# Row maxima of the attention scores from 64-row matmuls in two halves of the array

## The chip, the cores and the metric

The kernel runs on one core of a Trainium2 chip. The metric is the device time of one execution in microseconds (us). A profiled execution also has a span, the time from its first to its last instruction. TensorE is called PE here, VectorE DVE, ScalarE ACT, GpSimd POOL, and SyncE (which only issues transfers) SP. PE's weight loads have a row name of their own, PEld.

## The reference

Two layers of a transformer trunk work on 128 context tokens and 512 latent tokens of width 1024. Each layer has two groups of attention heads, then a gated feed-forward block. The change touches the attention alone, and of it this function and its twin:

```python
def diff_attend(q, k, v, lam):          # layer 0, 4 heads of two 64-wide maps each
    scale = q.shape[-1] ** -0.5
    def block(qb):
        s = jnp.einsum('bqhcd,bthcd->bhcqt', qb, k).astype(jnp.float32) * scale
        p = jax.nn.softmax(s, axis=-1)
        ...
def gqa_attend(q, k, v):                # layer 1, 8 query heads over 2 key heads, 64 wide
    ...
        s = jnp.einsum('bqkgd,btkd->bkgqt', qb, k).astype(jnp.float32) * scale
        p = jax.nn.softmax(s, axis=-1).astype(v.dtype)
```

For each latent query there are 640 keys (512 latent ones and 128 of a cache). A softmax is the same whatever number is subtracted from a row of scores, so the number that stands for the row's maximum may be a little off.

## The kernel before

**Numbers in two parts.** Most products run in the float32r type. A value is split in a high and a low part, and three products (high by high, high by low, low by high) are summed. For 64-wide heads the parts are stacked, so that one matmul over 128 rows of the array does two of the three: rows 0 to 63 of a tile `q1..` hold the high part, rows 64 to 127 the high part of q and the low part of k. A second tile `q2..` holds the rest and, in one extra row, the negated maxima.

**Pairs.** `attention` works through eight pairs per layer; a pair has two maps (`m` is 0 or 1). In layer 0 these are D0 to D3 (the differential heads) and M0 to M3 (96-wide latent heads); in layer 1 G0 to G3 (grouped-query heads) and N0 to N3 (neighbourhood heads, whose maxima take another path, `near`).

**Maxima.** `max_steps` gives eight steps for a pair, one for each map and each quarter `qt` of the 512 queries (function `one`). A step takes a PSUM tile `pm` of two banks, makes two matmuls of 320 keys each over all 128 rows with the same 128 queries as weights (L530), and DVE reduces 640 columns to one (L531). `fin` transposes the eight columns with one matmul (`pmx`), ACT negates them, and two small transfers (L554, `q<-att`) lay them into the extra row of the second tile.

**Scores and values.** The `st` tiles hold scores (L574, 512 queries wide), ACT takes their exponentials (L586), POOL sums them, and `po` tiles take the products with the values (L643). In layer 0's D pairs a `po` matmul has 128 output columns; in the M and G pairs it has 64, and the two maps stand in the two halves of the array's columns. `qs` (L719) holds the scores of the context tokens: 64 rows of the array, map 0 on rows 0 to 63, map 1 on rows 64 to 127. `ada` (L326) is filler work of the next modulation, 32 columns wide, with its weights in `wm`.

**Order.** The loop in `attention` mixes, by the strings in `CFG`, the maxima of pair i+1 (x), the scores of pair i (s) and the values of pair i-1 (v). A scheduler then orders each engine's instructions by their simulated readiness; PE, DVE, ACT, POOL and the SP queue each work in that order. The last two input projections of each layer (`peq`, `pek` in layer 0, `pnq`, `pnk` in layer 1; 128 rows, L186) run between the first pair's maxima. All transfers into the `q` tiles (L843 to L847 in `place64`, L1276 and L1277 for the G pairs) go through the SP queue (`PLACE`).

Of the kernel before, what the change touches and what calls it, by code (L numbers as in the profile page):

```python
# [11 lines left out]
F32R = mybir.dt.float32r  # L12
AF = mybir.ActivationFunctionType
ALU = mybir.AluOpType
AX = mybir.AxisListType
# [29 lines left out]
CFG = {"att0": ('xxsv', 4, 1, True, 2), "att1": ('vsxx', 4, 0, True, 2)}  # L45
TAIL = {"att0": 7, "att1": 9}
CUTS = {"op": 352, "dl": 352, "end": 384}
NCST = 5204
FULL = {5: 2, 8: 3}
KEEP = {5: 2, 8: 0}  # L50
NA_RANGES = [(0, 192), (64, 320), (192, 448), (320, 512)]
# [5 lines left out]
def tile_step(ctx: ExitStack, tc: tile.TileContext, a: dict):  # L57
    nc = tc.nc
    PE, ACT, DVE, POOL, SP = nc.tensor, nc.scalar, nc.vector, nc.gpsimd, nc.sync
# [7 lines left out]
    def dr(name, dt=F32):  # L67
        return dw(name, dt)[:, 0:1280]
# [4 lines left out]
    def d2(t):  # L73
        return t.rearrange("p (a b) -> p a b", a=2)

    def pmm(name):
        return pp.tile([128, 1024], F32, tag="mm", name=name, bufs=2)
# [3 lines left out]
    def psm(name, kind="sm"):  # L81

        tag, bufs = banks[kind]
        return pq.tile([128, 512], F32, tag=tag, name=name, bufs=bufs)
# [19 lines left out]
    def ring(tag, cols, bufs, dt=F32):  # L104

        if tag not in rings:
            rings[tag] = [0, [place([128, cols]) for _ in range(bufs)]]
        r = rings[tag]
        r[0] += 1
        v = r[1][(r[0] - 1) % bufs]  # L110
        return v if dt is F32 else v.bitcast(dt)
# [6 lines left out]
    def bf(t):  # L118
        return t.bitcast(F32)
# [6 lines left out]
    SPILL, SWAP, PLACE, OUT = POOL, ACT, SP, ACT  # L126
# [392 lines left out]

    def max_steps(pr):  # L520

        mx = ring("mx", 8, 2)

        def one(m, qt):
            mp = pr.maps[m]
            pt = pmm(f"pm{pr.name}{m}{qt}")
            ql = mp.qmax[:, qt * 128 : (qt + 1) * 128]
            col = mx[:, m * 4 + qt : m * 4 + qt + 1]
            for hf in range(2):
                PE.matmul(pt[:, hf * 512 : hf * 512 + 320], ql, mp.kmax[:, hf * 320 : hf * 320 + 320], start=True, stop=True)  # L530
            DVE.reduce_max(col, d2(pt)[:, :, 0:320], axis=AX.XY)  # L531

        def near(m, qts):

            mp = pr.maps[m]
            pt = pmm(f"pm{pr.name}{m}{qts[0]}")
            for i, qt in enumerate(qts):
                s, e = NA_RANGES[qt]
                n = e - s
                ql = mp.qmax[:, qt * 128 : (qt + 1) * 128]  # L540
                o = pt[:, 512 * i : 512 * i + 128 + n]
                PE.matmul(o[:, 0:128], ql, mp.kmax[:, 512:640], start=True, stop=True)
                PE.matmul(o[:, 128:], ql, mp.kmax[:, s:e], start=True, stop=False)
                PE.matmul(o[:, 128:], mp.ident, mp.combS[:, NA_COMB[qt] : NA_COMB[qt] + n], start=False, stop=True)
            c0, step = m * 4 + qts[0], qts[1] - qts[0]
            DVE.reduce_max(mx[:, c0 : c0 + step + 1 : step], d2(pt)[:, :, 0 : 128 + n], axis=AX.X)

        def fin():
            pm = psm(f"pmx{pr.name}")
            PE.matmul(pm[0:8, 0:128], mx, ident, start=True, stop=True)  # L550
            mr = pr.att.mr[pr.idx % 2][0:8].bitcast(F32R)
            ACT.activation(mr, pm[0:8, 0:128], AF.Copy, scale=-1.0)
            for m, mp in enumerate(pr.maps):
                PLACE.dma_start(bf(mp.maxrow), bf(mr[4 * m : 4 * m + 4, :]))  # L554

        if pr.na:
            return [lambda m=m, q=q: near(m, q) for m in range(2) for q in ((0, 3), (1, 2))], fin
        return [lambda m=m, qt=qt: one(m, qt) for m in range(2) for qt in range(4)], fin

    def score_steps(pr):  # L560
# [277 lines left out]

    def place64(slots, H, Lo, m):

        a1, a2 = slots.next()
        rs = slice(64 * m, 64 * m + 64)
        PLACE.dma_start(bf(a1[0:64, 0:1152]), H[rs, 0:1152])  # L843
        PLACE.dma_start(bf(a1[64:128, 0:512]), H[rs, 0:512])
        PLACE.dma_start(bf(a1[64:128, 512:1152]), Lo[rs, 512:1152])
        PLACE.dma_start(bf(a2[0:64, 0:512]), Lo[rs, 0:512])
        PLACE.dma_start(bf(a2[0:64, 512:1152]), H[rs, 512:1152])  # L847
        mp = Obj()
        mp.maxrow = a2[64:65, 0:512].rearrange("p (t q) -> p t q", t=4)
        mp.qmax, mp.kmax = a1[:, 0:512], a1[:, 512:1152]  # L850
        mp.passes = [(a1[:, 512:1152], a1[:, 0:512]), (a2[0:65, 512:1152], a2[0:65, 0:512])]
        return mp

    def new_pair(name, na, diff, dim, of):
        pr = Obj()
        pr.name, pr.na, pr.diff, pr.scale, pr.of = name, na, diff, dim ** -0.5, of
        pr.maps, pr.after = [], None
        return pr
# [53 lines left out]
    def mixer_even(u, o, fill, tail, pts):  # L912
# [9 lines left out]
        for j in range(4):  # L922
            t = {}
# [31 lines left out]
        pt = pmm("pkpe")  # L955
# [86 lines left out]
        for j in range(2):  # L1042
            cc = slice(512 + j * 128, 640 + j * 128)
            pt = pmm(f"pqr{j}")
# [67 lines left out]
        def mla_job(j):  # L1112
            def load():
                pr = new_pair(f"M{j}", False, False, 96, o[j])
                for m in range(2):
                    hd = 2 * j + m
                    a1, a2 = slots.next()
                    rs = slice(64 * m, 64 * m + 64)
                    rr = slice(32 * (hd % 4), 32 * (hd % 4) + 32)
                    qc = (hd // 4) * 512  # L1120
                    PLACE.dma_start(bf(a1[0:64, 0:1152]), mH[j][rs, 0:1152])
                    PLACE.dma_start(bf(a2[0:64, 0:1152]), mL[j][rs, 0:1152])
                    PLACE.dma_start(bf(a1[64:96, 0:512]), rH[rr, qc : qc + 512])
                    PLACE.dma_start(bf(a2[64:96, 0:512]), rL[rr, qc : qc + 512])
                    PLACE.dma_start(bf(a1[64:96, 512:1152]), kHL[:, 0:640])
                    PLACE.dma_start(bf(a2[64:96, 512:1152]), kHL[:, 640:1280])
                    DVE.memset(bf(a1[96:97, 512:1152]), 1.0)
                    mp = Obj()
                    mp.maxrow = a2[96:97, 0:512].rearrange("p (t q) -> p t q", t=4)
                    mp.qmax, mp.kmax = a1[0:96, 0:512], a1[0:96, 512:1152]  # L1130
                    mp.passes = [(a1[0:96, 512:1152], a1[0:96, 0:512]), (a2[0:96, 512:1152], a1[0:96, 0:512]), (a1[0:97, 512:1152], a2[0:97, 0:512])]
                    mp.ctx = [
                        (mctx[rs, j * 128 : j * 128 + 128], mctx[rs, 512 + j * 128 : 640 + j * 128]),
                        (mctx[rr, 1024 + (hd // 4) * 128 : 1152 + (hd // 4) * 128], kpc[rr, 0:128]),
                    ]
                    mp.v = lambda kt, hd=hd: vkt(vm, kt)[:, hd * 64 : hd * 64 + 64]
                    pr.maps.append(mp)
                return pr

            return load  # L1140
# [11 lines left out]
    def mixer_odd(raw, o, fill, tail, first, h):  # L1152
# [7 lines left out]
        gK = scratch("gK", [128, 1280])  # L1160
# [14 lines left out]
        for j in range(4):  # L1175
            t = {}
# [81 lines left out]
        kk, masks, lows = [], [], []  # L1258

        def gqa_job(j):  # L1260
            def load():
                if j == 0:
                    for g in range(2):
                        rs = slice(64 * g, 64 * g + 64)
                        t = dr(f"gk{g}", F32R)
                        PLACE.dma_start(bf(t[0:64, 0:640]), gK[rs, 0:640])
                        PLACE.dma_start(bf(t[64:128, 0:640]), gK[rs, 640:1280])
                        PLACE.dma_start(bf(t[0:64, 640:1280]), gK[rs, 0:640])
                        DVE.memset(bf(t[64:65, 640:1280]), 1.0)
                        kk.append(t)  # L1270
                pr = new_pair(f"G{j}", False, False, 64, o[j])
                g = j // 2
                for m in range(2):
                    rs = slice(64 * m, 64 * m + 64)
                    t, _ = slots.next(False)
                    PLACE.dma_start(bf(t[0:64, 0:1024]), gQ[j][rs, :])  # L1276
                    PLACE.dma_start(bf(t[64:128, 0:512]), gQ[j][rs, 0:512])  # L1277
                    mp = Obj()
                    mp.maxrow = t[64:65, 512:1024].rearrange("p (t q) -> p t q", t=4)
                    mp.qmax, mp.kmax = t[:, 0:512], kk[g][:, 0:640]  # L1280
                    mp.passes = [(kk[g][:, 0:640], t[:, 0:512]), (kk[g][0:65, 640:1280], t[0:65, 512:1024])]
                    mp.ctx = [(gctx[rs, 128 * j : 128 * j + 128], kctx[rs, 128 * g : 128 * g + 128])]
                    mp.v = lambda kt: vkt(vn, kt)[:, 512 + 64 * g : 576 + 64 * g]
                    pr.maps.append(mp)
                return pr

            return load
# [449 lines left out]
```

## Time and profile before

| what | value |
|---|---|
| time, median of 3 runs | 1895.18 us (1889.68, 1895.18, 1895.63) |
| time of the profiled execution | 1889.26 us |
| its span | 1887.1 us |
| PE busy | 1823.5 us, 97% of the span |
| DVE, ACT, POOL busy | 54%, 43%, 10% |
| mean granted TensorE clock | 0.975 of full speed |

The span and the profiled execution's time are to be read together (2.2 us lie around the span). PE's busy time counts matmuls with modelled ends, so a busy PE may still be waiting inside a row.

### The profile page before, as it was taken

To read this page: it belongs to the slowest core of one execution; us is meant where nothing else is said; L and a number is where in the kernel's file an instruction comes from. 1 tells how busy PE (TensorE), PEld (TensorE's weight loads), DVE (VectorE), ACT (ScalarE), POOL (GpSimd) and SP (SyncE) were. 2 spreads that over 40 slices of the span, in tenths; PEclk is the share of its full clock that TensorE was granted. 3 is DMA by queue.
4 is the path that set the end of the run, shared out by engine and by line. 5 is a ranking of instruction groups with operands and counts; after the bars stand their busy time and mean duration, and the time that the engine had idled before them with its cause. 6 is when DMAs were issued, how large, how long until landed. Compare 5 with 4: busy or idle time off the path is not lost. (4 is left out here: it accounts for less than half of the span.)

```text
span 1887.1 us, 29009 instructions
## 1 busy us (share of the span) xinstructions
PE 1823.5 (97%) x11715; PEld 1578.8 (84%) x11715; DVE 1014.7 (54%) x1782; ACT 803.6 (43%) x1325; POOL 190.2 (10%) x199
## 2 busy tenths in 40 slices
PE   7999799999999999999999999999999999999997
PEld 4888555559899999999989985455989999999996
DVE  3454445463774564663666654435377456466365
ACT  3433233345654452442475523324465444244244
POOL 0011243340000000000000003630000000000000
PEclk8999799999999999999999998999999999999998
DMA  7546555224223324333233364573412222222213
GB/s 283 167 147 224 140 173 143 77 95 162 79 85 97 126 78 145 128 114 107 97 101 131 131 197 141 162 200 114 168 68 100 91 68 67 82 75 62 85 58 105
DMA packets 84102, 229.88 MB, mean 122 GB/s; under 512 B 12225, under 2 KB 24897, under 8 KB 83969
## 3 DMA queue, kind: packets, MB, share of 16 engines
q1 hardware_dynamic: 74656, 209.73, 34.6%
q0 software_dynamic: 2592, 10.49, 1.5%
q10 hardware_dynamic: 6720, 7.82, 1.5%
q8 instruction: 92, 1.51, 0.3%
q14 instruction: 42, 0.34, 0.1%
HBM read 198.82 MB, written 28.06 MB: 120 GB/s over the span
## 5 line engine op out<-in xcount | busy, mean ns | idle before, releaser
L186 PE MATMUL pu<-uop,wh_u 128*128 128x322 f32 (+1 forms) x2688 | 512.6, 312 | 0.0
L186 PEld LDWEIGHTS pu<-uop,wh_u 128*128 128x128 f32 x2688 | 428.4, 190 | 5.8 <-ACT wh_u L160 4.1
L186 PE MATMUL pu<-uop,wl_u 128*128 128x322 f32 x1344 | 308.3, 311 | 0.0
L1361 DVE SCALAR_TENSOR_TENSOR za<-za,cst 128x127 f32<-128x127 f32 (+1 forms) x528 | 193.2, 435 | 92.1 <-ACT za L1353 91.8
L186 PEld LDWEIGHTS pu<-uop,wl_u 128*128 128x128 f32 x1344 | 224.8, 188 | 0.0
L186 PE MATMUL dn<-g,wh_d 128*128 128x320 f32 x1088 | 204.5, 309 | 0.1
L186 PEld LDWEIGHTS dn<-g,wh_d 128*128 128x128 f32 x1088 | 171.0, 188 | 0.9 <-ACT wh_d L160 0.9
L160 ACT ACTIVATE wh_u<-wr_u 128x1024 fp32r<-128x1024 f32 x88 | 92.9, 1058 | 138.3 <-PE dn L186 66.8
L271 POOL TENSOR_TENSOR cst<-cst 128x3 f32<-128x3 f32 (+2 forms) x23 | 24.8, 1077 | 1222.7 <-DVE cst L269 1220.0
L186 PE MATMUL dn<-g,wl_d 128*128 128x320 f32 x544 | 124.1, 309 | 0.0
L161 DVE TENSOR_TENSOR wl_u<-wr_u,wh_u 128x1024 fp32r<-128x1024 f32 x88 | 107.3, 1219 | 21.7 <-ACT wh_u L160 18.4
L442 ACT ACTIVATE za<-za,cst 128x128 f32<-128x128 f32 (+1 forms) x176 | 89.4, 555 | 38.3 <-DVE za L440 37.1
L186 PEld LDWEIGHTS dn<-g,wl_d 128*128 128x128 f32 x544 | 91.0, 188 | 0.0
L160 ACT ACTIVATE wh_d<-wr_d 128x768 fp32r<-128x768 f32 (+1 forms) x48 | 38.6, 809 | 103.8 <-PE dn L186 92.0
L1353 ACT ACTIVATE za<-za,cst 128x640 f32<-128x640 f32 x88 | 81.2, 923 | 3.0
L160 ACT ACTIVATE g<-za 128x640 fp32r<-128x640 f32 x44 | 32.5, 739 | 115.2 <-DVE za L1392 115.2
L439 DVE COPY cst<-pu 128x2 f32<-128x2 f32 x88 | 13.8, 157 | 123.7 <-PE pu L186 116.7
L1408 DVE TENSOR_TENSOR yf<-yf,dn 128x640 f32<-128x640 f32 x32 | 26.3, 821 | 94.8 <-PE dn L186 94.7
L1387 ACT ACTIVATE za<-za 128x640 f32<-128x640 f32 x44 | 32.5, 739 | 94.3 <-DVE za L1361 94.3
L440 DVE TENSOR_TENSOR za<-pu,rnuop 128x640 f32<-128x640 f32 x88 | 71.8, 816 | 0.0
L326 PE MATMUL ada<-wm,cst 128*32 128x256 f32 x768 | 64.0, 403 | 4.0 <-DMA wm<-in_wmod 2.0
L161 DVE TENSOR_TENSOR wl_op<-wr_op,wh_op 128x1024 fp32r<-128x1024 f32 x26 | 31.7, 1224 | 56.1 <-ACT wh_op L160 56.1
(585 smaller groups left out, 3424.2 us busy)
## 6 DMA issues: line engine op xcount, KB each, us to landing
wm<-in_wmod SPq DMA_DIRECT2D x96, 512.0 KB
wr_u<-in_w_up SPq DMA_DIRECT2D x88, 512.0 KB
wr_op<-in_w_o SPq DMA_DIRECT2D x26, 512.0 KB
wr_d<-in_w_dn SPq DMA_DIRECT2D x32, 384.0 KB
wr_dl<-in_w_dn SPq DMA_DIRECT2D x24, 320.0 KB
wr_d<-in_w_dn SPq DMA_DIRECT2D x16, 320.0 KB
h<-in_xT SPq DMA_DIRECT2D x4, 640.0 KB
hb<-in_xT SPq DMA_DIRECT2D x4, 640.0 KB
```

The lines of the kernel that those rows point to most:

```text
L160: ACT.activation(hi, src, AF.Copy)
L161: low.tensor_tensor(lo, src, hi, op=ALU.subtract)
L186: PE.matmul(o[hf], w, xhalf(x, hf, e), start=start, stop=stop)
L271: POOL.tensor_tensor(r[:, :nt], ms[:, :nt], mhalf.to_broadcast([128, nt]), op=ALU.pow)
L326: PE.matmul(st["pt"][32 * j : 32 * j + 32, 0:256], silu_c[:, 4 * r + j, :], st[r][:, j * 256 : (j + 1) * 256], start=(r == 0), stop=(r == 1))
L439: DVE.tensor_copy(zb, pt[:, 510 - cut : 512 - cut])
L440: DVE.tensor_tensor(dst, pview(pt, cut=cut), self.r, op=ALU.mult)
L442: ACT.activation(dst[:, s:e], dst[:, s:e], AF.Identity, bias=zb[:, ty : ty + 1])
L1353: ACT.activation(acc, z, AF.Identity, scale=cw[:, 1:2], bias=cw[:, 3:4])
L1361: DVE.scalar_tensor_tensor(acc[:, d0 : d0 + n], z[:, s0 : s0 + n], w, acc[:, d0 : d0 + n], op0=ALU.mult, op1=ALU.add)
L1387: ACT.activation(t[0], t[0], AF.Silu)
L1408: DVE.tensor_tensor(yv, yv, pview(pt), op=ALU.add)
```

## The change

Of a map of 64 rows the maximum is now taken from the product of the high parts alone, which needs 64 rows of the array instead of 128. Map 0 takes rows 0 to 63, map 1 rows 64 to 127. A step (function `both`) makes, for one quarter of the queries and one half `hf` of the keys, one matmul for each map, into the two banks of a `pm` tile, and DVE reduces it to two columns (one for each map). The eight steps of a pair leave 16 columns in a new ring `mh`; one DVE instruction takes the larger of the two key halves ahead of the transposing matmul. It is done for D0 to D3 and G0 to G3. M pairs (96 wide) and N pairs keep their own functions.

So that map 1's high parts stand on rows 64 to 127, `place64` lays its first tile the other way round, and for the G pairs a new tile `gk2` holds the keys' high part on the upper rows: two transfers more on the SP queue.

```diff
-NCST = 5204
+NCST = 5236
...
-        mx = ring("mx", 8, 2)
+        mx, mh = ring("mx", 8, 2), ring("mh", 16, 2)
...
+        def both(qt, hf):
+
+            pt = pmm(f"pm{pr.name}{qt}{hf}")
+            for m, mp in enumerate(pr.maps):
+                q, k = mp.hh
+                PE.matmul(pt[:, m * 512 : m * 512 + 320], q[:, qt * 128 : (qt + 1) * 128], k[:, hf * 320 : hf * 320 + 320], start=True, stop=True)
+            DVE.reduce_max(mh[:, 8 * hf + qt : 8 * hf + qt + 5 : 4], d2(pt)[:, :, 0:320], axis=AX.X)
...
         def fin():
+            if pr.maps[0].hh and not pr.na:
+                DVE.tensor_tensor(mx, mh[:, 0:8], mh[:, 8:16], op=ALU.max)
             pm = psm(f"pmx{pr.name}")
...
+        if pr.maps[0].hh:
+            return [lambda qt=qt, hf=hf: both(qt, hf) for qt in range(4) for hf in range(2)], fin
         return [lambda m=m, qt=qt: one(m, qt) for m in range(2) for qt in range(4)], fin
...
-        PLACE.dma_start(bf(a1[0:64, 0:1152]), H[rs, 0:1152])
-        PLACE.dma_start(bf(a1[64:128, 0:512]), H[rs, 0:512])
-        PLACE.dma_start(bf(a1[64:128, 512:1152]), Lo[rs, 512:1152])
+        other = slice(64 - 64 * m, 128 - 64 * m)
+        PLACE.dma_start(bf(a1[rs, 0:1152]), H[rs, 0:1152])
+        PLACE.dma_start(bf(a1[other, 0:512]), H[rs, 0:512])
+        PLACE.dma_start(bf(a1[other, 512:1152]), Lo[rs, 512:1152])
...
+        mp.hh = (a1[rs, 0:512], a1[rs, 512:1152])
...
+                    t = dr("gk2", F32R)
+                    for g in range(2):
+                        PLACE.dma_start(bf(t[64:128, 640 * g : 640 * g + 640]), gK[64 * g : 64 * g + 64, 0:640])
+                    kk.append(t)
...
+                    mp.hh = (t[rs, 0:512], kk[2][rs, 640 * g : 640 * g + 640] if m else kk[g][rs, 0:640])
```

The order of PE's instructions moves with it. The first place is PE where the maxima of D3 run beside the scores of D2 and the values of D1, before the change (`pmD300` is pair D3, map 0, quarter 0; `q010` and `q011` are the first tiles of maps 0 and 1 of that pair):

```order
L530 MATMUL pmD300_1984<-q010_1462 128x320 x2
L333 MATMUL ada011_1927<-cst_69 128x2 x2
L530 MATMUL pmD301_1988<-q010_1462 128x320 x2
L643 MATMUL poD10_2002<-psD1_1831,vd2_1304 128x512
L574 MATMUL stD200_1994<-q014_1660 128x512
L643 MATMUL poD11_2003<-psD1_1831,vd2_1304 128x512
L530 MATMUL pmD302_2010<-q010_1462 128x320 x2
```

The same place after the change (`pmD301` is now quarter 0, key half 1; the line numbers are those of the changed kernel):

```order
L538 MATMUL pmD300_1987<-q010_1462 128x320
L538 MATMUL pmD300_1987<-q011_1470 128x320
L333 MATMUL ada011_1929<-cst_69 128x2 x2
L538 MATMUL pmD301_1991<-q010_1462 128x320
L758 MATMUL qoD1_1967<-att0_1459,vd0_1302 128x128
L655 MATMUL poD10_2005<-psD1_1833,vd2_1304 128x512
L538 MATMUL pmD301_1991<-q011_1470 128x320
L586 MATMUL stD200_1997<-q014_1661 128x512
```

The two matmuls of a step stand next to each other, but for one step (`pmD301`), which is parted by two matmuls of 128 rows; the neighbours of the steps are matmuls of 128 rows and 128 columns, as before.

The second place is PE where the maxima of G2 run, before the change:

```order
L643 MATMUL poG00_10141<-psG0_10003,vn2_9645 64x512
L530 MATMUL pmG200_10154<-gk1_9611,q114_9993 128x320 x2
L326 MATMUL ada110_10171<-wm1100_10137,cst_69 32x256 x4
L326 MATMUL ada110_10171<-wm1101_10139,cst_69 32x256 x4
L530 MATMUL pmG201_10158<-gk1_9611,q114_9993 128x320 x2
L643 MATMUL poG00_10141<-pG000_10010,vn0_9643 64x512
```

And after it:

```order
L655 MATMUL poG00_10150<-psG0_10011,vn2_9652 64x512
L538 MATMUL pmG200_10163<-gk1_9615,q114_10001 128x320
L538 MATMUL pmG200_10163<-gk2_9620,q115_10004 128x320
L326 MATMUL ada110_10180<-wm1100_10146,cst_69 32x256 x4
L326 MATMUL ada110_10180<-wm1101_10148,cst_69 32x256 x4
L538 MATMUL pmG201_10167<-gk1_9615,q114_10001 128x320
L538 MATMUL pmG201_10167<-gk2_9620,q115_10004 128x320
L655 MATMUL poG00_10150<-pG000_10018,vn0_9650 64x512
```

Here the neighbours are matmuls of 64 or 32 columns before and after, so that the array's shape changed on both sides of a step already.

The third place is the SP queue ahead of the maxima of D1, before the change (`q012` and `q013` are the first tiles of D1's maps 0 and 1, `q020` and `q021` the second tiles of D0, `q014` that of D2):

```order
L843 DMA q012_1643<-dH1_501 64x1152
L845 DMA q012_1643<-dL1_505 64x640
L844 DMA q012_1643<-dH1_501 64x512
L843 DMA q013_1651<-dH1_501 64x1152
L554 DMA q020_1463<-att0_1459 1x4x128
L845 DMA q013_1651<-dL1_505 64x640
L844 DMA q013_1651<-dH1_501 64x512
L843 DMA q014_1660<-dH2_502 64x1152
```

And after it (L857 is the former L843, L859 the former L845, L564 the former L554):

```order
L857 DMA q012_1644<-dH1_501 64x1152
L564 DMA q020_1463<-att0_1459 1x4x128
L564 DMA q021_1471<-att0_1459 1x4x128
L857 DMA q013_1652<-dH1_501 64x1152
L857 DMA q014_1661<-dH2_502 64x1152
L857 DMA q015_1669<-dH2_502 64x1152
L859 DMA q012_1644<-dL1_505 64x640
```

The negated maxima of D0 now go out ahead of the first transfer into `q013`, and the low parts of D1 behind the high parts of D2.

## Rows read from the trace of the kernel before

**Rows 1.** The page's busy time, share of the span and instructions of PE.

```profile
PE 1823.5 (97%) x11715; PEld 1578.8 (84%) x11715; DVE 1014.7 (54%) x1782; ACT 803.6 (43%) x1325; POOL 190.2 (10%) x199
```

**Rows 2.** Stretches: length, busy PE, PEld, DVE, ACT, POOL; granted clock, DMA share, GB/s.

```profile
215.00:231.00 16.00, 12.71 (x49) 9.59 (x53) 12.80 (x19) 5.53 (x7) 7.04 (x7) 0.59 0.82 241
231.00:296.00 65.00, 63.95 (x302) 35.48 (x290) 33.31 (x59) 25.80 (x44) 31.10 (x25) 1.00 0.55 155
1137.00:1157.00 20.00, 16.30 (x73) 11.00 (x72) 9.38 (x16) 7.45 (x11) 5.37 (x4) 0.66 0.67 185
1157.00:1232.00 75.00, 72.65 (x363) 33.43 (x361) 32.89 (x55) 25.89 (x47) 45.84 (x51) 1.00 0.52 156
```

**Rows 3.** PE's waits from 231 to 296 us: only the heading.

```profile
engine line waited for: us in total, times, longest us
```

**Rows 4.** Timeline of PE, layer 0's last projections: start, length, instructions, [idle before].

```profile
187.39 0.75 PE L186 MATMUL peq<-u,wh_eq 128*128 128x320 f32 x4
187.97 0.46 PE L186 MATMUL peq<-u,wl_eq 128*128 128x320 f32 x2
188.27 0.75 PE L186 MATMUL peq<-u,wh_eq 128*128 128x320 f32 x4
...
204.15 0.28 PE L550 MATMUL pmxD<-cst 128*8 128x128 f32 x1 [1.35 <-DVE cst L531]
```

**Rows 5.** DVE's instructions by form, 1115 to 1300 us: count, busy us, mean ns.

```profile
L531 DVE TENSOR_REDUCE cst<-pmG 128x1 f32<-128x640 f32 x32 | 25.7, 821 | 44.8 <-PE pmG L530 44.8
L546 DVE TENSOR_REDUCE cst<-pmN 128x2 f32<-128x640 f32 x8 | 6.6, 823 | 4.9 <-PE pmN L544 4.8
L354 DVE TENSOR_TENSOR cst<-cst 128x8 f32<-128x8 f32 x2 | 0.4, 218 | 0.0
```

**Rows 6.** Stretches of 30 ns, of tile qsD, then of qsM: columns as Rows 2.

```profile
261.66:261.69 0.03, 0.02 (x2) 0.02 (x2) 0.00 (x0) 1.00 2.68 358
...
346.82:346.85 0.03, 0.02 (x1) 0.02 (x1) 0.00 (x0) 1.00 0.00 0
```

**Rows 7.** Timeline of PE around a 64-row block at full clock.

```profile
284.19 1.88 PE L643 MATMUL poD<-pD,vd 128*128 128x512 f32 x4
286.00 0.49 PE L719 MATMUL qsD<-dctx 64*128 64x128 f32 x4
286.42 0.56 PE L530 MATMUL pmM<-q 96*128 96x320 f32 x2
286.82 0.59 PE L643 MATMUL poD<-pD,vd 128*128 128x512 f32 x1
```

**Rows 8.** Timeline of PE in D1, at the lower clock.

```profile
223.85 0.80 PE L719 MATMUL qsD<-dctx 64*128 64x128 f32 x4
224.58 1.43 PE L530 MATMUL pmD<-q 128*128 128x320 f32 x4
225.81 1.05 PE L574 MATMUL stD<-q 128*128 128x512 f32 x2
226.67 1.27 PE L530 MATMUL pmD<-q 128*128 128x320 f32 x4
227.73 1.78 PE L574 MATMUL stD<-q 128*128 128x512 f32 x6
```

**Rows 9.** Timeline of PE in G2: from 128 to 64 columns.

```profile
1171.74 0.46 PE L530 MATMUL pmG<-gk,q 128*128 128x320 f32 x2
1172.12 1.08 PE L643 MATMUL poG<-pG,vn 128*64 128x512 f32 x4
```

**Rows 10.** Timeline at D1's start: SP's issues (SPq) and PE.

```profile
209.44 0.45 SPq L844 DMA_DIRECT2D q<-dH  x1
...
215.04 0.45 SPq L843 DMA_DIRECT2D q<-dH  x1
...
215.19 1.40 PE L530 MATMUL pmD<-q 128*128 128x320 f32 x4 [7.75 <-DMA q<-dH]
215.58 0.70 SPq L554 DMA_DIRECT2D q<-att  x1
...
219.50 1.65 PE L574 MATMUL stD<-q 65*128 65x512 f32 x3 [2.48 <-DMA q<-att]
```

**Rows 11.** SP's longest wait ahead of D1's second tile.

```profile
SPq L843 <- DVE dqk L905: 5.1, 1, 5.1
```

More of the change, by code (lines that the diff above doesn't have):

```diff
@@ L1130, in load @@
                     mp.qmax, mp.kmax = a1[0:96, 0:512], a1[0:96, 512:1152]
+                    mp.hh = None
                     mp.passes = [(a1[0:96, 512:1152], a1[0:96, 0:512]), (a2[0:96, 512:1152], a1[0:96, 0:512]), (a1[0:97, 512:1152], a2[0:97, 0:512])]
```

## The prediction

> **What bounds the kernel now.** I read the page first: PE is busy for 97% of the span, the next engine for 54% [rows 1]. Then the two stretches in which the changed matmuls lie, cut where the granted clock changes [rows 2]. From 231 to 296 us (D2, D3) PE is busy for 63.95 of 65 us, from 1157 to 1232 us (G1 to G3) for 72.65 of 75, DVE and ACT for about half of it at most, all at full clock (2.4 GHz). The list of PE's waits for the first of these is empty [rows 3]. There a nanosecond less or more on PE moves the end. In the two other stretches, D1 and G1 after a long wait, the clock is 0.59 and 0.66 on average, which means that much of them ran at 1.2 GHz. Last I read single rows, since busy PE time includes what happens between two matmuls, and that is where this change has its price.
>
> **What is taken away.** A matmul of 320 columns in a dense stream costs 0.147 us: six of them lie between 187.39 and 188.27 [rows 4]. At the lower clock four take 226.67 to 227.73, 0.265 each [rows 8]. The number of matmuls stays (two for each of 64 steps), so the gain is only what two of them overlap. That they can is seen in `qs`, which already uses both halves of the rows: in a window of 30 ns two matmuls and two weight loads of `qsD` are under way, where `qsM`, with both maps' parts issued on one row half at a time, shows one [rows 6]. Four `qsD` then fill 0.42 us in all (286.00 to 286.42, [rows 7]). I take full overlap, 0.147 us saved for a step. By PE's order 60 of the 64 steps have a partner to overlap with: D301 is parted, and in D0, D1 and G1 one run issues map 0 twice, then map 1 twice, which overlaps one time instead of two. Of the 60, 12 lie at the lower clock (seven of D1, five of G1), 33 in the dense stretches (15 of D2 and D3, 18 of G1 to G3), and 15 in D0 and G0. Without D0 and G0: 33 x 0.147 + 12 x 0.265 = 8.0 us less.
>
> **What is added: changes of the array's shape.** Wherever PE goes from 128 rows to 64 or back, or from 128 columns to 64 or 32, there is a hole. Around one block of `qs` [rows 7]: the four `po` matmuls take 1.88 us with the last one's whole 0.59, so one fills (1.88 - 0.59) / 3 = 0.43, and the last slot ends at 284.19 + 4 x 0.43 = 285.91. `qs` starts at 286.00, and the two matmuls of 320 columns behind it end their slots at 286.82. Between 285.91 and 286.82 there is 0.91 us, in which two overlapped rounds of `qs` (128 of the 512 columns of `po`, 0.107 each) and two slots of 0.147 are work, 0.51 together. The other 0.40 us are two changes, 0.20 each. Half of it is a drain (285.91 to 286.00), half a weight load that nothing covers: the first matmul behind a change is longer by it. At the lower clock the same count gives about 0.30: from 223.85 to 225.81 there are 1.96 us with 0.43 of `qs` and 1.06 of maxima, 0.47 left, and one drain of 0.13 ahead of it [rows 8]. Into 64 columns the drain is the same (1171.74 to 1172.12 is 0.38 for two slots of 0.29, [rows 9]) and the load shorter: between 0.09 and 0.20, and I take 0.13 for 64 and 32 columns.
>
> The Trainium skill has the rule that speaks against this change: "TensorEngine Tiling (Array Packing)", section "Key Properties", says that changing the tiling mode, not merely the tile, drains TensorE. The trace agrees (0.09 us of drain in rows 7 and 9) and adds the load; the page gives no price.
>
> Counted over PE's whole order, the shape changes 457 times before and 502 after. D0 has 5 more, G0 6 more, D1 to D3 26 more (29 more into 128 columns, 3 fewer into 32), G1 to G3 9 more (13 more into 128, 4 fewer into 64 and 32). In layer 0 a step mostly stands between matmuls of full shape and pays twice; in layer 1 it often stands next to `po` or `ada`, where the shape changed anyway, and a step next to `qs` pays nothing. Price without D0 and G0: 42 x 0.20 - 7 x 0.13 = 7.5 us; ten of them lie at the lower clock, 0.10 dearer each, 1.0. Together 8.5 us. Against 8.0 saved that is +0.5.
>
> **D0 and G0.** Their steps stand in the projections: 15 x 0.147 = 2.2 saved, 11 x 0.20 = 2.2 paid, nothing. It is no more either way, since four steps in a row wait for PSUM that DVE frees at 0.82 us a step.
>
> **The reductions.** Two columns out of 640 instead of one: 823 against 821 ns [rows 5], nothing. The one instruction that joins the halves is 128x8, 0.22 us [rows 5]; eight of them lie on DVE, half idle. In D0 and G0 alone PE waits for the last reduction (1.35 us before `pmx`, [rows 4]), and the new one lies in that chain: 2 x 0.22 = +0.4.
>
> **Transfers.** D1's first maxima now need map 1's first tile too. Before, they waited until 215.19 for the third transfer into map 0's tile, issued at 209.44; map 1's first transfer was issued at 215.04, since SP stood 5.1 us behind DVE's L905, which frees its memory [rows 10, 11]. That wait stays where it is in the SP queue. The transfer of the maxima issued right behind it, at 215.58, landed so that PE went on at 219.50, 3.9 us later [rows 10]; I give map 1's tile the same, landing near 218.7. Two steps (three slots of 0.265 and two changes of 0.30) then end near 220.1. D0's negated maxima are earlier in the queue, so the scores follow without their wait; before, one of four scores was done and the next began at 219.50. Loss: 1.0 us. Against it, fewer bytes stand ahead of the transfer on which L905 waits, which may bring L905 forward by up to 1.5 us. Bounds -0.7 and +1.3, I take +0.5. G1's two tiles are issued next to each other and were the last thing waited for already; `gk2` has some 20 us of slack: nothing.
>
> **Sum.** +0.5 + 0.4 + 0.5 = +1.4 us. The profiled execution took 1889.26, which would become 1890.7; the median of the three runs is 5.9 above it, 1895.18, so the time is 1896.6. From no change this can't be told: 0.3%, 5.7 us, is about what a measurement of this kernel can tell, and its three runs before lie 5.95 apart.
>
> **Bounds.** A change at the drain alone (0.09, 0.13 at the lower clock) makes 3.6 instead of 8.5, the sum -3.5. No overlap leaves the price alone, the sum +9.4.
>
> **Rivals.** *The changes are hidden.* The drain and the exposed load fall into waits that the trace does not name, and the overlap comes through: -8.0 + 0.9 = -7.1, 1888. For it: ends of matmuls are modelled, and PEld is busy for only 35 of 65 us. Against it: the hole in rows 7 lies in a stretch without a wait.
>
> The Trainium skill's page "TensorEngine Tiling (Array Packing)", section "Theoretical Speedup", gives up to twice the rate for 64 rows, which is this rival.
>
> *The pairs do not overlap.* `qs` is plain float32 of 128 columns; no row shows two float32r matmuls of 320 columns side by side. If the second waits for the first, 8.5 + 0.9 = +9.4 remain, 1904.6: slower. It decides once less than 3.7 of the 8.0 us come. Against it are the starts within 30 ns [rows 6].
>
> *The start of D1.* The high parts of D2 now stand right behind map 1's tile in the queue, and PE idles longer after the 7.75 us of before. If the tile lands 2 us later than I think and the lower clock holds for 5 us of work longer (2.5 lost), the sum is 1.4 + 4.5 = +5.9, 1901. Against it: the bytes ahead are fewer than before.
>
> **Chances.** Forecast (within some 4 us of before) 0.62; changes hidden 0.16; no overlap 0.12; D1's start 0.10. Faster by over 0.3% is the first rival, 0.16; slower the other two, 0.22; within 0.3% 0.62. The range goes from just below the first rival to just below the second, 1887 to 1903, which also covers the spread of the runs; the forecast's own is 1890 to 1901.
>
> **What would show it.** Right: pairs of `pm` matmuls starting within 10 ns; a lone pair between full-shape matmuls filling about 0.55 us against 0.29 before; the stretch of D2 and D3 some 2 to 3 us longer, that of G2 and G3 some 1 us shorter; PE waiting until near 218.5 for the first maxima of D1 and no wait for `q<-att` behind them. Wrong: pair starts 147 ns apart; runs of two pairs filling 0.3 us; a wait of PE for DVE in the dense stretches; a lower clock beyond 231 us.

## The result

The changed kernel takes 1899.49 us (median of 22 runs, 1889.86 to 1907.18) against 1888.93 us (22 runs, 1883.07 to 1895.63): ratio 1.0053, 95% interval 1.0039 to 1.0067. The range of the prediction (1887 to 1903) holds the time. Its likeliest case, no measurable change, does not hold: the kernel is slower by about 10 us.

The runs of one kernel lie far apart, and each comes with its mean granted clock: 1889.97 us at 0.974, 1907.18 at 0.963. The profiled execution is that slowest one. The page of the kernel after, PE's busy time [rows 1] and the granted clock in 40 slices of the span:

```profile
PE 1840.0 (97%) x11715; PEld 1575.6 (83%) x11715; DVE 1018.1 (53%) x1790; ACT 804.9 (42%) x1325; POOL 189.7 (10%) x199
...
PEclk8999799999999999999999996988999999999998
```

The same line of the page of before:

```profile
PEclk8999799999999999999999998999999999999998
```

The dip in the middle is layer 1's attention. To find the place I cut both executions at the same instructions: D0 (end of `pvd` to `pmxD`), the start of D1 (to the first `qoD`), D2 and D3 (to `bcD1b`), then the start of G1 (end of `pnk` to the first `qoG`), G2 and G3 (to `suG`), and the N pairs (to the last `qtN`). Columns as in [rows 2]. Before:

```profile
185.03:204.15 19.12, 17.56 (x115) 16.51 (x113) 6.17 (x8) 2.73 (x5) 0.40 (x1) 1.00 0.15 45
204.15:233.39 29.24, 16.96 (x86) 12.09 (x87) 16.75 (x24) 7.62 (x12) 7.57 (x8) 0.65 0.77 214
233.39:299.88 66.49, 65.23 (x312) 36.41 (x310) 35.38 (x61) 25.33 (x44) 34.22 (x27) 1.00 0.56 159
1137.80:1160.37 22.57, 18.87 (x91) 12.37 (x89) 11.16 (x19) 9.41 (x14) 6.64 (x5) 0.70 0.60 164
1160.37:1211.29 50.92, 49.46 (x234) 21.91 (x234) 19.82 (x36) 16.56 (x31) 30.48 (x31) 1.00 0.51 151
1211.29:1303.99 92.70, 89.13 (x573) 50.04 (x573) 42.25 (x70) 28.92 (x57) 29.48 (x44) 0.96 0.63 180
```

After:

```profile
184.36:203.91 19.55, 17.38 (x115) 15.52 (x113) 6.30 (x9) 2.73 (x5) 0.40 (x1) 1.00 0.16 47
203.91:230.76 26.85, 19.33 (x85) 11.19 (x86) 16.28 (x25) 7.62 (x12) 7.53 (x8) 0.56 0.80 225
230.76:298.18 67.42, 66.61 (x312) 33.72 (x311) 37.89 (x63) 25.62 (x44) 33.47 (x27) 1.00 0.56 155
1138.96:1167.34 28.38, 22.60 (x93) 12.47 (x91) 12.38 (x21) 9.77 (x14) 6.93 (x6) 0.58 0.52 147
1167.34:1221.62 54.28, 51.45 (x233) 21.06 (x232) 20.92 (x37) 16.89 (x30) 29.83 (x31) 0.87 0.48 142
1221.62:1323.63 102.01, 96.93 (x574) 54.12 (x573) 42.24 (x70) 28.92 (x57) 29.43 (x44) 0.87 0.56 159
```

The three stretches of layer 0 are together 1.0 us shorter (19.55 + 26.85 + 67.42 = 113.82 against 114.85). Layer 1 loses 18.5 us in three stretches, and in all three the granted clock is lower: 0.58 for 0.70, 0.87 for 1.00, 0.87 for 0.96. The N pairs, 9.3 us of it, are not touched by the change. D1 started earlier, at 213.26 and 214.42 us for its two tiles instead of 215.19, and the wait for `q<-att` behind it [rows 10] is gone:

```profile
213.26 0.87 PE L538 MATMUL pmD<-q 64*128 64x320 f32 x2 [6.16 <-DMA q<-dH]
214.42 0.90 PE L538 MATMUL pmD<-q 64*128 64x320 f32 x2 [0.29 <-DMA q<-dH]
215.25 2.07 PE L586 MATMUL stD<-q 128*128 128x512 f32 x4
```

### The profile page after: what moved, and what is told of

The parts are those of the page before. It is cut to its first block, busy times and chain, and to the rows that moved or that the text cites. A ratio compares the mean times of both kernels' runs of the same rounds, so it can differ in the third digit from the quotient of the medians.

```text
span 1905.1 us, 29023 instructions
## 1 busy us (share of the span) xinstructions
PE 1840.0 (97%) x11715; PEld 1575.6 (83%) x11715; DVE 1018.1 (53%) x1790; ACT 804.9 (42%) x1325; POOL 189.7 (10%) x199
```

## The experiments

Three theories: **shape** (the lower clock goes with the 64-row matmuls), **late tile** (it goes with the longer waits at the starts of D1 and G1, where a step now needs both maps' tiles), **chance** (the low stretches move about in every kernel alike). The table has all timed kernels; "clock" is the mean over a kernel's executions, the last two columns are read from its profile, cut as above. A ratio is to the executions of before that were timed beside the kernel, so it differs a little from the quotient of two medians of the table. There are 22 executions of after and of before (87 for its clock), 6 of no_overlap, 5 of holes, and 12 of every other kernel.

| kernel | 64-row steps in | median us | ratio to before (95%) | clock | G2, G3 | N |
|---|---|---|---|---|---|---|
| before | none | 1888.93 | 1 | 0.977 | 1.00 | 0.96 |
| after | D, G | 1899.49 | 1.0053 (1.0039 to 1.0067) | 0.969 | 0.87 | 0.87 |
| again | D, G | 1900.91 | 1.0060 (1.0040 to 1.0081) | 0.968 | 1.00 | 0.90 |
| d_only | D | 1894.04 | 1.0020 (0.9997 to 1.0043) | 0.974 | 1.00 | 0.96 |
| g_only | G | 1897.72 | 1.0036 (1.0015 to 1.0056) | 0.971 | 0.84 | 0.90 |
| moves | none | 1889.63 | 0.9997 (0.9975 to 1.0019) | 0.977 | 1.00 | 0.93 |
| both128 | none | 1897.02 | 1.0039 (1.0019 to 1.0058) | 0.975 | 1.00 | 0.96 |
| no_overlap | D, G | 1906.19 | 1.0088 (1.0061 to 1.0115) | 0.967 | 0.81 | 0.91 |
| holes | none | 1907.79 | 1.0118 (1.0098 to 1.0137) | 0.975 | 0.94 | 0.94 |
| warm_before | none | 1887.18 | 0.9989 (0.9975 to 1.0002) | 0.983 | 1.00 | 0.93 |
| warm_after | D, G | 1893.24 | 1.0022 (1.0003 to 1.0041) | 0.974 | 0.90 | 0.91 |
| warm_d | D | 1884.71 | 0.9984 (0.9970 to 0.9999) | 0.982 | 1.00 | 0.96 |
| warm_g1 | none | 1888.33 | 1.0009 (0.9986 to 1.0032) | 0.978 | 1.00 | 0.93 |

**again** is the changed kernel without an edit.

> The changed kernel once more, for a second profile and more executions. Shape theory (the granted clock falls, or stays low longer, because PE works on half of its rows): ratio 1.003 to 1.007, mean granted clock below 0.972 in most executions. Late-tile theory (G1's first maxima wait 2.5 us instead of 0.9 for their tiles, and the clock stays low behind it): the same ratio, and the low stretch that begins at 1143 us ends late only where this wait is long. Chance theory (the low stretches move about in every kernel): clock of before spread as widely, 0.963 to 0.975.

The ratio repeats. This execution (1896.68 us, clock 0.973) has the same low stretch in G1 as before, none in G2 and G3, and a longer one in the N pairs; the start of G1, G2 and G3, N:

```profile
1139.26:1164.41 25.15, 18.65 (x92) 10.38 (x91) 12.39 (x21) 9.65 (x14) 6.41 (x5) 0.73 0.59 166
1164.41:1212.47 48.06, 45.38 (x233) 19.58 (x233) 20.93 (x37) 16.83 (x31) 30.43 (x31) 1.00 0.51 150
1212.47:1313.26 100.79, 94.76 (x574) 52.98 (x573) 42.25 (x70) 28.96 (x57) 29.45 (x44) 0.90 0.60 166
```

With no more low clock than before, G1 to G3 take 25.15 + 48.06 = 73.21 us against 73.49. Chance falls: of the 87 executions of before timed beside the experiments two are at a mean clock of 0.970 or lower, of the changed kernel's 34 it is 27. Late tile finds no support either: G1's wait for its tiles is 3.0 us here, longer than the 2.5 of the first profile, and the low stretch behind it is 17 us shorter.

**d_only** and **g_only** make one half of the change each. In d_only (which loads no `gk2` either):

```diff
-                    mp.hh = (t[rs, 0:512], kk[2][rs, 640 * g : 640 * g + 640] if m else kk[g][rs, 0:640])
+                    mp.hh = None
```

In g_only (which lays the tiles of `place64` as before):

```diff
-        mp.hh = (a1[rs, 0:512], a1[rs, 512:1152])
+        mp.hh = None
```

> The change for D0 to D3 alone; G0 to G3 as before, without the tile gk2. Shape and late-tile theory, with the loss placed in layer 1: -1 to -3 us (the first profile after the change was 1.3 us ahead of before from M0 on), clock 0.973 to 0.976. If the shape lowers the clock wherever it is used: part of the loss stays, +2 to +5 us. Chance theory: the clock spreads as in the changed kernel.

> The change for G0 to G3 alone; D0 to D3 as before. Shape and late-tile theory: the whole loss, +8 to +13 us, clock below 0.972 in most executions, and a low stretch behind the start of G1 that lasts 20 us or more. Chance theory: about half of the loss.

The two halves add up: 0.0020 and 0.0036 of time (3.8 and 6.8 us), 0.003 and 0.005 of clock. So neither half has the whole loss: g_only misses its +8 to +13 us, and d_only lies within its +2 to +5. That layer 0 pays is clear by the clock (0.974 against 0.977 of before) and not by the time alone, since d_only's interval just includes no loss. d_only spreads from 1882.94 us at 0.979 to 1898.33 at 0.971, and its profile is of an execution near the short end (1885.51 us, 0.976).

**moves** keeps the transfers and the layout and computes the maxima as before (both `mp.hh = None`).

> The data laid out as in the change (map 1's first tile the other way round, the two transfers into gk2), but all maxima computed as before from 128 rows; gk2 is loaded and not used. Shape theory: within 2 us of before, clock 0.973 to 0.976. Late-tile theory: within 2 us as well if the delay comes from the first step needing both tiles, +5 to +10 us if it comes from the transfers ahead in the queue.

Time and clock of before. The transfers and their order cost nothing, also with 1.7 us of wait for `q<-gQ` at G1.

**both128** has the steps of the change at full height:

```diff
-                q, k = mp.hh
+                q, k = mp.qmax, mp.kmax
```

> The changed kernel with its steps, its order, its transfers and its joined maxima, but each matmul of a step over all 128 rows again, as before (so two matmuls of a step no longer overlap, and the array's shape doesn't change at a step). If the 64-row matmuls bring the lower clock: mean granted clock 0.976 to 0.978 as before, and within 3 us of before (0.4 us for the joining instruction, up to 2 for the waits at the starts of D1 and G1). If the waits at those starts bring it (both tiles are needed at once): clock 0.967 to 0.972 and +5 to +12 us.

Neither side is met as a whole. The time is that of late tile, but from waits of this kernel's own: a 128-row step also needs the other rows of its tiles, which stand later in the queue now, so that D0 takes 23.64 us instead of 19.12, and G1 waits 4.9 us for `q<-gQ`. In G2 and G3, where no tile is waited for, it is a clean comparison. There the clock stays at full:

```profile
1168.01:1216.68 48.67, 46.24 (x233) 21.54 (x232) 21.00 (x37) 16.87 (x31) 30.47 (x31) 1.00 0.48 145
```

The first profile of the changed kernel has the same order of PE and the same waits there as both128 (both128's are 0.64, 0.69 and 0.43 us). Here its clock falls; timeline of PE in G3, and the stretch that begins within the last of these rows:

```profile
1203.02 0.41 PE L538 MATMUL pmG<-gk,q 64*128 64x320 f32 x2
1204.19 0.41 PE L538 MATMUL pmG<-gk,q 64*128 64x320 f32 x2 [0.76 <-ACT pG L598]
1204.53 0.73 PE L586 MATMUL stG<-q,gk 128*128 128x512 f32 x2
1205.95 0.62 PE L326 MATMUL ada<-wm,cst 128*32 128x256 f32 x2 [0.69 <-ACT psG L598]
...
1210.17 0.41 PE L538 MATMUL pmG<-gk,q 64*128 64x320 f32 x2
1211.01 0.41 PE L538 MATMUL pmG<-gk,q 64*128 64x320 f32 x2 [0.43 <-ACT pG L598]
1211.51 2.26 PE L586 MATMUL stG<-q,gk 128*128 128x512 f32 x5
```

```profile
1211.82:1218.65 6.83, 6.83 (x26) 2.34 (x28) 1.23 (x3) 2.04 (x4) 4.27 (x4) 0.50 0.24 66
```

These two profiles alone do not decide, for `again` stays at 1.00 in G2 and G3 too. All profiles together say more: of the five with 64-row steps in G four have a low stretch there (0.81 to 0.90), of the eight without only holes (0.94). So do the executions: with the same steps both128 has a mean clock of 0.975, the changed kernel 0.969 and 0.968.

**no_overlap** puts both maps' high parts on rows 0 to 63.

```diff
+        mp.hh = (a1[0:64, 0:512], a1[0:64, 512:1152])
...
+                    mp.hh = (t[0:64, 0:512], kk[g][0:64, 0:640])
```

> The changed kernel with both maps' high parts on rows 0 to 63: the same 64-row matmuls and the same changes of the array's shape, but the two of a step follow each other. By the sum of the prediction 60 pairs lose their overlap, 33 x 0.147 + 12 x 0.265 + 15 x 0.147 = 10.2 us, so +8 to +12 us over the changed kernel (+18 to +23 over before) if the clock stays where the change put it; less, +6 to +12 over before, if the clock of before comes back with the longer steps.

At a pair's start one matmul is under way instead of two (windows of 30 ns of tile pmD, no_overlap and then after; length, PE, PEld, DVE, clock):

```profile
240.46:240.49 0.03, 0.03 (x1) 0.03 (x1) 0.00 (x0) 1.00 0.54 205
```

```profile
234.75:234.78 0.03, 0.03 (x2) 0.03 (x2) 0.00 (x0) 1.00 0.97 273
```

It costs 5.3 to 6.7 us over the changed kernel (by the two medians of that kernel), less than the 8 to 12 expected: D2 and D3 take 69.23 us, 1.81 more than in after, where 15 pairs at 0.147 make 2.2; where the rest of the 10.2 us went was not followed up. The clock doesn't come back with the longer steps. And it is the counterpart of both128: G1 waits only 0.6 us for its tile, and still the start of G1 and then G2 and G3 have the lowest clocks of all kernels:

```profile
1143.68:1171.88 28.20, 25.31 (x93) 14.63 (x91) 12.09 (x21) 9.88 (x14) 6.94 (x6) 0.55 0.55 152
1171.88:1230.82 58.94, 57.02 (x234) 24.87 (x233) 20.86 (x37) 16.99 (x30) 29.82 (x31) 0.81 0.43 128
```

PE's waits for G1's tiles (total, times, longest), in both128, no_overlap and again:

```profile
PE pmG L538 <- DMA q<-gQ: 4.9, 1, 4.9
PE pmG L538 <- DMA q<-gQ: 0.6, 1, 0.6
PE pmG L538 <- DMA q<-gQ: 3.0, 2, 1.7
```

Late tile falls with the first two: 4.9 us of wait at full height leave the clock of G2 and G3 at 1.00, 0.6 us at half height go with 0.81, and over all executions the mean clocks are 0.975 and 0.967.

**holes** separates the changes of shape from the 64-row work:

```diff
                 PE.matmul(pt[:, hf * 512 : hf * 512 + 320], ql, ...
+                if hf == 0 and pr.name[0] in "DG":
+                    PE.matmul(pt[:, 320:328], ql[0:64], mp.kmax[0:64, 0:8], start=True, stop=True)
```

> The kernel before with one small matmul more in each of the 64 steps of D and G, between the two of 320 columns: 64 rows, 128 x 8, into columns that nothing reads. It makes two changes of the array's shape per step and next to no work. By the prediction's price (0.20 us a change): 64 x 0.40 = +26 us at an unchanged clock, of which 16 x 0.40 = 6.4 us in D2 and D3 (from the first value product to the last of the D pairs). If the holes at the changes are what the lower clock goes with: a low stretch within G2 and G3 (where the kernel before has none), mean granted clock 0.965 to 0.972, and +29 to +36 us. If it goes with the 64-row work itself: clock 0.975 to 0.978, +23 to +28 us.

The price is in the timeline of PE, first in D0 at full clock, then in D1 at the lower one:

```profile
204.09 0.31 PE L530 MATMUL pmD<-q 128*128 128x320 f32 x1
204.33 0.27 PE L532 MATMUL pmD<-q 64*128 64x8 f32 x1
204.53 0.56 PE L530 MATMUL pmD<-q 128*128 128x320 f32 x2
205.02 0.27 PE L532 MATMUL pmD<-q 64*128 64x8 f32 x1
...
226.68 0.37 PE L532 MATMUL pmD<-q 64*128 64x8 f32 x1
226.98 0.90 PE L530 MATMUL pmD<-q 128*128 128x320 f32 x2
227.81 0.37 PE L532 MATMUL pmD<-q 64*128 64x8 f32 x1
```

From one small matmul to the next there are 0.69 us with two slots of 0.147: 0.40 for two changes, 0.20 each. At the lower clock 1.13 with two of 0.265: 0.60, 0.30 each. The Trainium skill, "TensorEngine Tiling (Array Packing)", section "Key Properties", has the drain without a price; these rows are the price with the load behind it. The whole costs 18.7 us by the medians (22 by the ratio), not 26. A part of the difference is seen in its profile: in D0 the steps wait for PSUM anyway (+1.9 us of 3.2), and D2 and D3 pay 5.6 of 6.4, which is 0.18 for a change. The clock, 0.975 (0.971 to 0.979), is slightly below that of before and well above 0.969. Its 0.94 in G2 and G3 is the end of G1's low stretch, at 1184.32 us; that stretch, and what follows:

```profile
1153.60:1184.32 30.72, 29.02 (x81) 15.23 (x79) 8.48 (x14) 6.78 (x11) 10.19 (x8) 0.50 0.50 129
1184.32:1236.24 51.92, 51.17 (x241) 24.58 (x240) 19.65 (x36) 15.32 (x27) 26.45 (x28) 1.00 0.46 135
```

So 128 changes of shape more (the changed kernel has 45 more) bring 0.002 of the mean clock, where the changed kernel loses 0.008. The larger part goes with the 64-row work. That the changes bring a part is not excluded: these are five executions, and in the profile, which is of the slowest of them (0.971), G1's low stretch is 30.7 us long, as in after, against 13.7 before.

**warm_before**, **warm_after**, **warm_d** and **warm_g1** add idle work ahead of D1 and G1 (40 and 10 matmuls; 0 and 10 in warm_g1), on before, after, d_only and before:

```diff
+        mp, pt = prs[0].maps[0], psm(f"warm{name}")
+        for _ in range(WARM[name]):
+            w = PE.matmul(pt[:, 0:320], mp.qmax[:, 0:128], mp.kmax[:, 0:320], start=True, stop=True)
+            tc.add_manual_dep(w.ins, prs[0].neg.ins.name, AFTER)
```

> The kernel before with idle work added: after the first pair's negated maxima PE repeats one matmul of 128 x 320, 40 times in layer 0 (5.9 us at full clock) and 10 times in layer 1, into a bank that nothing reads. PE waits there 7.75 us anyway [rows 10]. If the idle time brings the low clock of D1: the low stretch of 207 to 228 us ends earlier or is not there, -3 to -8 us. If not: 0 to +3 us.

> The changed kernel with the same idle work. If the part of the loss that comes with D0 to D3 (3 to 4 us) is the low clock of D1 lasting longer: -6 to -11 us against the changed kernel, and a smaller distance to the kernel before with the same idle work. If the loss is spread over later stretches: -3 to -8 us as for before, the distance unchanged at 10 us.

In warm_before the idle work fills the wait of D1, and the 20 us of low clock there shrink to 3.4 and 6.8; the stretch behind G1's start is gone (19.45 us at full clock instead of 22.57 at 0.70). Its timeline of PE at D1, and its stretch from `pnk` to `qoG`:

```profile
205.15 7.66 PE L781 MATMUL warmatt<-q 128*128 128x320 f32 x40 [1.40 <-ACT att L553]
212.74 0.62 PE L327 MATMUL ada<-wm,cst 128*32 128x256 f32 x2
```

```profile
1139.95:1159.40 19.45, 15.84 (x101) 10.39 (x100) 11.74 (x19) 9.30 (x14) 6.47 (x5) 1.00 0.70 191
```

It gains 2 to 3 us, which the interval just doesn't part from nothing. In its profile a part is lost again: the scheduler puts D2 and D3 in another order, and they take 69.18 us instead of 66.49. On the changed kernel the same work gains 6 to 8 us, so that 4 us (0.0022) to before are left of 10; the clock rises from 0.969 to 0.974. To warm_before 6.1 us remain, which is the smaller distance of the first expectation, but not all of the loss: G2 and G3 keep a low stretch (0.90).

> The change for D0 to D3 alone, with the idle work of 40 and 10 matmuls. From the first profiles: D takes 111.6 us with it instead of 114.9 before, the start of G1 19.5 instead of 22.6. -4 to -8 us against before (ratio 0.996 to 0.998), clock 0.980 to 0.984. If the low clock of D1 was not what the change cost in D: no better than the kernel before with the same idle work, 0 to -3 us.

> The kernel before with 10 idle matmuls ahead of G1 and none in layer 0. If the low clock of G1 (13.7 us long before) begins with PE's waits there: no low stretch behind 1140 us, -2 to -5 us, clock 0.979 to 0.981. Otherwise +1 to +2 us.

warm_d is just faster than before: 1884.71 us, ratio 0.9984, interval 0.9970 to 0.9999. That is less than the expected 4 to 8 us and can't be told from warm_before (0.9989), so no gain from the D half of the change itself is shown. Of the 3.1 us that warm_before's profile gained at the start of G1, warm_g1's shows 0.8 (21.80 us, clock 0.92), and its time shows no gain (1.0009): its N pairs took 96.53 us at 0.93.

## Why the prediction's range held and its difference did not

**Luck.** The range held the time partly by luck. The forecast started from 1895.18 us, the median of three executions, where 22 have 1888.93. The difference was missed by 9.2 us, the time only by 2.9, because the start was 6.2 too high.

**The pairs overlap** as forecast, and where single rows show the price of a change of shape it is the forecast one, 0.20 and 0.30 us. **The reductions** are as long as before [rows 5], and the joining instruction has its 0.2 us. DVE's instructions by form, after:

```profile
L539 DVE TENSOR_REDUCE cst<-pmG 128x2 f32<-128x640 f32 x32 | 25.6, 821 | 46.0 <-PE pmG L538 45.6
...
L558 DVE TENSOR_TENSOR cst<-cst 128x8 f32<-128x8 f32 x4 | 0.8, 210 | 0.1
```

**D0 and G0** pay more for it than the forecast 0.22 us each: PE's wait ahead of `pmx` goes from 1.35 to 1.80 us in D0, which is 0.43 us longer, and from 1.21 to 1.45 in G0.

**D2 and D3** are 0.9 us longer. Each of the two stretches has a wait in it, before 1.2 us for ACT near its end, after 0.7 us for DVE's reduction (one of the signs of being wrong); without them it is 1.4. Counted over PE's order between these cuts there are 23 more changes into 128 columns and 2 fewer into 32, so the forecast terms give 23 x 0.20 - 2 x 0.13 - 15 x 0.147 = 2.1. Over a whole stretch the price of a change was thus put somewhat too high, as holes shows too (0.18).

**G1 to G3** are 0.3 us shorter in the execution with the clock of before. G2 and G3, for which about 1 was forecast, are 2.9 shorter, but both128, with the same order of PE at full height, takes 48.67 us there, so that only 0.6 of it is the overlap's. The start of G1 is 2.6 us longer: its first maxima wait 3.0 us for their tiles instead of 0.9, a term that the prediction put at nothing.

**D1's start** was forecast as a loss of 0.5 us (bounds -0.7 and +1.3), with map 1's tile landing near 218.7 us (215.04 and 3.9 would make 218.9). PE went on with that tile at 214.42 us in after and at 217.87 in again, and the wait for `q<-att` is gone as forecast. The stretch, 29.24 us before, is 2.4 us shorter in after, 2.9 in d_only and as long in again, so two of three profiles gain more than the bounds allow. D_only and again:

```profile
203.66:229.98 26.32, 18.32 (x86) 10.46 (x86) 16.30 (x25) 7.62 (x12) 7.54 (x8) 0.61 0.81 230
204.96:234.19 29.23, 18.98 (x86) 10.96 (x86) 16.30 (x25) 7.62 (x12) 7.54 (x8) 0.59 0.74 207
```

**The sum** thus came near by terms that missed in both directions. At an equal clock it holds to 3 or 4 us: the changed kernel's six executions at 0.973 and 0.974 have a mean of 1892.2 us, before's eight of these clocks 1894.4, so -2.2 where +1.4 was forecast.

**The step that failed** is one that the sum took for granted. "There a nanosecond less or more on PE moves the end" was said of stretches at full clock, and the sum left every stretch at the clock that it had before. The missing term is that clock. A straight line through the 87 executions of before has 14.8 us for 0.01 of mean clock, through the changed kernel's 34 it is 15.4. The mean clock falls from 0.9766 to 0.9684: 0.82 x 14.8 = 12.1 us. With the -2.2 at equal clock that makes +9.9; the means of the executions differ by 10.3. This is an estimate, since such a line need not hold for another kernel: warm_before, at 0.983, lies 7.5 us above before's line.

**Rivals.** "The changes are hidden" is refuted by holes, "the pairs do not overlap" by the two windows. "The start of D1" had the mechanism, a low stretch that lasts longer, but at one place and for 0.10: layer 0 has 3.8 us of the loss by d_only, 6.8 us are layer 1's, where the prediction asked only about waits for tiles. The prediction's sign of being wrong, "a lower clock beyond 231 us", came true in layer 1.

**What stays open.** Why the N pairs, which the change leaves alone, run at 0.87 to 0.91 in all five profiles with 64-row steps in G and at 0.93 to 0.96 in all eight without. The longer of their low stretches in after begins within a wait of PE for the weights of `ada`. Timeline, and the stretch with its clock:

```profile
1288.59 0.28 PE L624 MATMUL slN<-cb,cl 128*128 128x256 f32 x1
1291.95 1.08 PE L326 MATMUL ada<-wm,cst 128*32 128x256 f32 x8 [3.07 <-DMA wm<-in_wmod]
```

```profile
1290.33:1307.39 17.06, 15.44 (x60) 7.84 (x61) 3.70 (x9) 2.20 (x4) 0.00 (x0) 0.50 0.44 156
```

Before, the longest such wait is 1.3 us. But moves (2.4 us) and warm_g1 (3.0) wait as long and stay at 0.93, so the wait is not the whole cause. In layer 0 the cause is not parted from the waits and the order of the steps: d_only and both128 have nearly the same clock (0.974 and 0.975). Whether the fewer rows count or the halved work of a step is open too, since no run has shorter matmuls over 128 rows. And the runs do not show by what rule the clock is granted; they show in which kernels and stretches it fell.

## What to carry to other kernels

Price a packing into half of the array's rows by the changes of shape around it: here a pair of 320 columns saves 0.147 us and a change costs 0.20, so a step that pays for two loses, and one that stands where the shape changed anyway gains. Then ask for each stretch what happens to the granted clock, read it for many executions and not for one profile, and compare executions of two kernels at equal clock before blaming an instruction. Where PE waits for a transfer anyway, idle matmuls in that wait can be tried: here they gained 6 to 8 us on the changed kernel, and 2 to 3, not clear of noise, on the one before.

## What the hardware showed unasked

The same kernel, before any change, spreads from 0.970 to 0.983 in mean clock and from 1881.5 to 1904.36 us in 87 executions. 64-row matmuls that follow each other (no_overlap, 0.967) run at a clock as low as pairs that overlap (0.969), while the same steps at 128 rows hold 0.975 in spite of longer waits. A change of shape costs half as much again at the lower clock (0.30 us against 0.20).
